# Two-layer hybrid backbone on one core: two-piece modulation steps, part of layer 1's modulation in its own mixer, last gathered products issued during expert selection

## The chip, the cores and the metric

The kernel runs on one core of a Trainium2 chip. The metric is the device time of one execution in microseconds (us); the median of several runs is compared. The engines are TensorE (PE: matmuls; PEld: its weight loads), VectorE (DVE), ScalarE (ACT), GpSimd (POOL) and SyncE (SP). DMA transfers are issued from queues that belong to engines: SP loads weights, ACT loads some activations, POOL issues the indirect transfers that gather rows by index.

## What is computed

Two layers over 256 latent tokens and 256 context tokens, width 1024, all in float32. Cut to what matters:

```python
mod = silu(c) @ w_mod[l] + b_mod[l]          # 6 vectors of 1024; one set for latent, one for context
h = rmsnorm(x) * (1 + scale1) + shift1       # mod 0, 1
x = x + mod[2] * token_mixers(h)             # one input projection, four mixers, merge, output projection
h = rmsnorm(x) * (1 + scale2) + shift2       # mod 3, 4
x = x + mod[5] * peer_ffn(h)                 # layer 0 also for the context tokens
def peer_ffn(t):                             # per token, 8 heads
    q = t @ w_q                              # product-key scores: two top-16, then top-16 of 256 sums
    e, g = chosen 128 experts, softmax gates
    act = gelu(u_tab[e] . t)
    return sum(g * act * v_tab[e])           # 16384 experts per layer
```

## The kernel before

The program is one list of items (class Item: a function and the weight pieces that it reads). `run` (line 92) goes through the list once and writes out the instructions of all engines in that order; each engine then executes its own instructions in order. Ahead of each item `load` (line 100) issues the next weight pieces of 512 KB on SP. Pieces that are cut into two fp32r halves go through three `raw` buffers; pieces with a `ring` name go, in order, through the buffers of `self.ring`, as soon as `ring_for` has their name and a buffer is free. `cut` (line 167) makes the halves on ACT and on DVE or POOL. FIRST (line 71) is the item before which no cut is made ahead of need.

**Modulation** (`mod_items`, line 322). `w_mod` of a layer is 48 pieces: three groups (group 0: vectors 0 and 1; group 1: 2 and 3; group 2: 4 and 5), four quarters q, four pieces kp. One piece is one step: two matmuls with 512 columns (line 356), each of which writes 32 of the 128 partitions of a PSUM tile psM; the profile shows two records for each matmul. After four steps ACT copies the row (line 363), TensorE transposes it (line 334), and DVE adds it up (lines 336 to 346). Layer 0: group 0 runs at the start of the program, groups 1 and 2 are woven among the input products and scans of its mixer (line 988) through a ring of four buffers. Layer 1: all 48 steps stand in layer 0's expert stage, woven among six query products and the first nine up steps (line 1550), through four buffers.

**Expert stage** (`peer`, line 1005). The latent tokens (in layer 1 their last 160) take the dense way: every expert of the layer is multiplied with all of them. The other 256 (layer 0: the context tokens) or 96 tokens are "far": their chosen rows are gathered. The order is:

- Seven query items (`wq`, line 1101), with the head scores and top-k on DVE beside them.
- 128 up steps (`up`, line 1312): eight matmuls (line 1318) with a piece of `peer_u`, and GELU on ACT. Beside them, as *row products*: POOL gathers one row of `u_rows` per token into a buffer of 512 KB (line 1217), and DVE multiplies and adds it up against the tokens (line 1248), 256 times in layer 0, 96 in layer 1, with six other buffers fetched ahead in layer 0.
- N/4 selection items (`experts`, line 1354; 64 in layer 0, 40 in layer 1): one-hot matrices from ACT, DVE and POOL (`one_hots`, line 1328; lines 1343 to 1349), four products that place the gates (line 1361), and a DVE product (line 1363).
- 128 down steps (`down`, line 1475; products of line 1498 in layer 1, of `mm3`, lines 200 to 202, in layer 0) with `peer_v`. The far tokens' down part (`far_down`, line 1376) gathers four rows at a time and needs eight matmuls (line 1409, psC) per step; 64 steps in layer 0, 24 in layer 1. EARLY (line 84) of these steps are spread over the selection items: 24 in layer 0, none in layer 1.

What stands beside an item is set by a budget written out by hand. `routing` (line 1276) is a generator that yields the cost of each thing that it issues (1.3 for a row product, 0.1 + n/700 for one top-k instruction on n values, and so on); `aside` (line 1303) adds the item's allowance to `due` and draws from the generator until `due` is used up. The allowances are WQ = 8.0 per query item and UP = 4.3 per up step in layer 0, 3.5 and 1.9 in layer 1. In `beside`, SHARE (0.75 in layer 0) is the part of other routing work that is drawn for each product. At up step 111 the own tokens' gates must be complete; at up step 127 of layer 0 all that is left is issued (1e6). Line 1290 lets `routing` wait, before the first row product of layer 0, until all 48 modulation steps are issued:

```python
            while two and hold["mods"] < 48:
                yield None
```

In layer 0, `far_steps` begins with selection item 0; in layer 1 after the last one. The transpose of line 1259, which follows the last row product of a tile, stands in TensorE's order where the budget puts it.

Of the kernel before, what the change touches and what calls it, by code (L numbers as in the profile page):

```python
# [6 lines left out]
F = mybir.dt.float32  # L7
# [62 lines left out]
class Builder:  # L70
    RAW, CUT, AGE, FIRST = 3, 5, 2, 20
# [12 lines left out]
    FAR, WQ, UP, SHARE, EARLY = (256, 96), (8.0, 3.5), (4.3, 1.9), (0.75, 0.6), (24, 0)  # L84
# [237 lines left out]
    def mod_items(self, l, groups, tag=("O", 1), turn=("T", 2), rows=("u", 1), ring="mix"):  # L322
# [25 lines left out]
        def fn(g, q, kp):  # L348
            def go(p):
                if kp == 0:  # L350
                    hold["ps"] = self.ps.tile([128, 512], F, tag=tag[0], name="psM", bufs=tag[1])
                ps = hold["ps"]
# [5 lines left out]
                if kp == 3:  # L358
                    row, (rt, n) = [], rows
                    for i in range(n):  # L360
                        w = 512 // n
                        rw = self.mp.tile([128, w], F, tag=rt, name="row", bufs=2)
                        nc.scalar.activation(rw, ps[:, i * w:i * w + w], AF.Copy)
# [3 lines left out]
        return [Item(fn(g, q, kp), Piece(self.t["w_mod"][l, g, q, kp], 1024, split=False, ring=ring))  # L367
                for g in groups for q in range(4) for kp in range(4)]

# [39 lines left out]
    def mixer(self, l, need):  # L409
# [14 lines left out]
        def begin():  # L424
# [42 lines left out]
        def ring_end():  # L467

            del self.ring[4:]
            self.ring_for = "mix"  # L470
# [497 lines left out]
        if l == 0:  # L968
            m = self.mod_items(l, (0,), tag=("A", self.BANKS["A"]), turn=("T", self.BANKS["T"]), ring="start")
            seq += m[:1] + [Item(stats1)] + m[1:4]  # L970
            seq += [Item(lambda: squares_end(0, 4)), m[4], Item(norm1), norm_steps(2)]
            seq += m[5:9] + [norm_steps(2)]
            seq += m[9:13] + [norm_steps(2)] + m[13:] + [Item(ring_end), self.lo(l, 0), Item(self.flush), norm_steps(3)]
# [5 lines left out]
        mods = self.mod_items(l, (1, 2), tag=("T", self.BANKS["T"]), turn=("T", self.BANKS["T"])) if l == 0 else []  # L979
# [25 lines left out]
    def peer(self, l, seg, far):  # L1005
# [270 lines left out]
        def routing():  # L1276
# [13 lines left out]
            while two and hold["mods"] < 48:  # L1290
                yield None
# [6 lines left out]
            yield from r  # L1298

# [12 lines left out]
        def up(i):  # L1312
            def fn(p):
# [7 lines left out]
                aside(self.UP[l] if i < 127 or not two else 1e6, "own" if i == LAST - 1 else None)  # L1321
# [31 lines left out]
        def experts(t4):  # L1353

            def fn():
# [184 lines left out]
        if l < L - 1:  # L1540
            def one(it):
                def fn(p):
                    it.fn(p)
                    hold["mods"] += 1
                    if hold["mods"] == 48:
# [119 lines left out]
```

## Time and profile before

| what | us |
|---|---|
| median of 3 runs (lowest, highest) | 3461.22 (3460.14, 3463.15) |
| profiled execution, its own time | 3454.95 |
| span of it, first to last instruction | 3453.2 |

Layer 0's mixer takes the span up to about 780, its expert stage to 2190 (up steps to 1493, selection to 1682, down steps to 2190), layer 1's mixer to 2690, its expert stage to 3453 (up steps to 3053, selection to 3109). The profile was taken in one execution. "Busy" is the time in which an engine had an instruction under way; an arrow in a row of waits points to what ended the wait; "x" is a count of records. Matmul ends are modelled and overlap, so the distance of starts tells more than one record's length. DMA share is the mean over the core's 16 DMA engines.

### The profile page before, as it was taken

What the parts mean: (1) busy time and instruction counts of PE and PEld (TensorE: products, weight loads), DVE (VectorE), ACT (ScalarE), POOL (GpSimd) and SP (SyncE); (2) the same over time, 40 slices, a digit from 0 to 9 for tenths busy, and PEclk for the clock granted to TensorE, in tenths of its full rate; (3) what the DMA queues carried; (4) which work ended last, traced back from release to release, by engine and by line L of the source; (5) the groups of instructions that cost most, each with busy time, mean ns of one, the idle gap of its engine ahead of it and who ended that gap; (6) DMA issues with size and microseconds to landing.
All of it is one profiled execution on the core that took longest, in us unless ns stands there. A gap on an engine that the chain in (4) does not pass through costs nothing. (4 is left out here: it accounts for less than half of the span.)

```text
span 3453.2 us, 50801 instructions
## 1 busy us (share of the span) xinstructions
PE 3152.3 (91%) x19130; PEld 2516.4 (73%) x19130; DVE 1890.9 (55%) x4591; ACT 1073.5 (31%) x2268; POOL 1259.8 (36%) x1178
## 2 busy tenths in 40 slices
PE   7999999997879999678888999899999899989998
PEld 4667766785458877543566889777878799888887
DVE  5557444445389999655433446677444767670001
ACT  4544444331101011034332335564454110160000
POOL 2422222220044445557434550344454033473330
PEclk9999999998989999899999999999999999999999
DMA  7522212334789999968778996523234699939996
GB/s 262 168 89 62 64 57 65 92 110 160 262 314 369 386 371 395 408 232 277 251 282 324 393 395 195 164 86 92 84 107 146 201 348 409 404 133 361 378 376 213
DMA packets 245013, 819.03 MB, mean 237 GB/s; under 512 B 31776, under 2 KB 50464, under 8 KB 244512
## 3 DMA queue, kind: packets, MB, share of 16 engines
q1 hardware_dynamic: 137824, 441.40, 36.8%
q0 software_dynamic: 101376, 369.14, 28.6%
q10 hardware_dynamic: 5568, 5.24, 0.5%
q8 instruction: 151, 2.47, 0.3%
q14 instruction: 94, 0.77, 0.1%
HBM read 809.37 MB, written 6.29 MB: 236 GB/s over the span
## 5 line engine op out<-in xcount | busy, mean ns | idle before, releaser
L178 POOL TENSOR_TENSOR whl<-raw,whl 128x512 fp32r<-128x512 f32 x249 | 325.7, 1323 | 829.9 <-ACT whl L174 764.5
L1318 PE MATMUL psA<-hb,raw 128*128 128x256 f32 x2048 | 474.2, 391 | 12.9 <-DMA raw<-peer_u 9.4
L176 DVE TENSOR_TENSOR whl<-raw,whl 128x512 fp32r<-128x512 f32 x359 | 272.5, 767 | 375.3 <-ACT whl L174 311.2
L174 ACT ACTIVATE whl<-raw 128x512 fp32r<-128x512 f32 x608 | 362.7, 627 | 322.0 <-PE acc L202 241.4
L1318 PEld LDWEIGHTS psA<-hb,raw 128*128 128x128 f32 x2048 | 394.0, 196 | 90.5 <-issue 19.1
L200 PE MATMUL psA<-hhi,whl 128*128 128x512 f32 (+1 forms) x1032 | 376.4, 365 | 10.0 <-ACT hhi L504 5.3
L202 PE MATMUL psA<-hhi,whl 128*128 128x512 f32 (+1 forms) x1032 | 364.2, 353 | 2.7 <-DVE whl L176 2.4
L201 PE MATMUL psA<-hlo,whl 128*128 128x512 f32 (+1 forms) x1032 | 365.4, 354 | 1.3 <-POOL hlo L505 1.2
L1217 POOL DMA_INDIRECT fetched<-u_rows,ft x184 | 184.1, 1001 | 333.5 <-DVE ft L1176 142.1
L200 PE MATMUL acc<-wh,whl 128*128 128x256 f32 x1024 | 295.3, 288 | 2.9 <-ACT wh L205 2.9
L201 PE MATMUL acc<-wh,whl 128*128 128x256 f32 x1024 | 290.8, 284 | 2.2 <-DVE wh L206 2.2
L202 PE MATMUL acc<-wh,whl 128*128 128x256 f32 x1024 | 290.4, 284 | 0.0
L1320 ACT ACTIVATE A<-psA 128x512 f32<-128x512 f32 (+1 forms) x128 | 66.2, 517 | 721.1 <-PE psA L1318 615.4
L1248 DVE SCALAR_TENSOR_TENSOR fetched<-fetched,hT 128x1024 f32<-128x1024 f32 x184 | 222.0, 1210 | 31.6 <-DMA fetched<-u_rows,ft 17.8
L200 PEld LDWEIGHTS psA<-hhi,whl 128*128 128x128 f32 x1032 | 198.5, 192 | 54.6 <-issue 18.7
L200 PEld LDWEIGHTS acc<-wh,whl 128*128 128x128 f32 x1024 | 197.2, 193 | 38.1 <-issue 14.9
L202 PEld LDWEIGHTS psA<-hhi,whl 128*128 128x128 f32 x1032 | 198.1, 192 | 30.4 <-DVE whl L176 3.6
L201 PEld LDWEIGHTS psA<-hlo,whl 128*128 128x128 f32 x1032 | 197.9, 192 | 27.5 <-POOL hlo L505 1.8
L1217 POOL DMA_INDIRECT hb<-peer_v,ft x140 | 145.6, 1040 | 176.0 <-PE psC L1409 142.1
L201 PEld LDWEIGHTS acc<-wh,whl 128*128 128x128 f32 x1024 | 197.5, 193 | 2.4 <-DVE wh L206 2.4
L202 PEld LDWEIGHTS acc<-wh,whl 128*128 128x128 f32 x1024 | 197.4, 193 | 0.0
L1217 POOL DMA_INDIRECT own<-u_rows,ft x96 | 105.7, 1101 | 241.1 <-DMA fetched<-peer_u 97.8
(372 smaller groups left out, 6065.7 us busy)
## 6 DMA issues: line engine op xcount, KB each, us to landing
raw<-peer_u SPq DMA_DIRECT2D x176, 512.0 KB
raw<-peer_v SPq DMA_DIRECT2D x176, 512.0 KB
raw<-w_in SPq DMA_DIRECT2D x126, 512.0 KB
fetched<-peer_u SPq DMA_DIRECT2D x80, 512.0 KB
fetched<-peer_v SPq DMA_DIRECT2D x80, 512.0 KB
ring<-w_mod SPq DMA_DIRECT2D x72, 512.0 KB
raw<-w_branch SPq DMA_DIRECT2D x32, 512.0 KB
hb<-w_mod SPq DMA_DIRECT2D x24, 512.0 KB
```

The source lines that it names most:

```text
L174: nc.scalar.activation(hx, x, AF.Copy)
L176: nc.vector.tensor_sub(lx, x, hx.bitcast(F))
L178: nc.gpsimd.tensor_sub(lx, x, hx.bitcast(F))
L200: mm(ps, wh, xh, start=start, stop=False, skip_group_check=skip)
L201: mm(ps, wh, xl, start=False, stop=False, skip_group_check=skip)
L202: mm(ps, wl, xh, start=False, stop=stop, skip_group_check=skip)
L1217: nc.gpsimd.indirect_dma_start(out=buf, out_offset=None, in_=rows, in_offset=bass.IndirectOffsetOnAxis(ap=idx.bitcast(I32), axis=0))
L1248: nc.vector.scalar_tensor_tensor(b, b, 1.0, h, op0=OP.mult, op1=OP.mult, accum_out=f[:, 3, k:k + 1])
L1318: nc.tensor.matmul(ps[:, :N], p.raw[:, k * 128:k * 128 + 128], h32[:, k, off:], start=k == 0, stop=k == 7)
L1320: nc.scalar.activation(A[:, i - 1:i + 1, :], hold["ps"][:, :, :N], AF.Gelu_apprx_tanh)
```

## The change

- A modulation step takes two pieces and issues four matmuls, one for each quarter of the partitions; a group has 8 steps instead of 16.
- Layer 1's groups 1 and 2 move from layer 0's expert stage into layer 1's mixer, woven among its input products and scans as in layer 0, through a ring of two buffers (the tiles `ohi` and `olo`); the row is copied in two parts into tiles with the tag `u`. Group 0 stays, woven among the query items only; line 1290 waits for its 8 steps, and all up steps follow.
- UP of layer 0 is 4.0 instead of 4.3. At up step 127 the rest is no longer issued at once: selection items draw 2.5 each until the row products are through, and the last draws all. `far_steps` begins at the item at which they are through, and catches up by at most one step per item. EARLY of layer 1 is 6 instead of 0, so that six of its 24 far down steps stand in the selection.
- FIRST is 14 instead of 20.

```diff
-    RAW, CUT, AGE, FIRST = 3, 5, 2, 20
+    RAW, CUT, AGE, FIRST = 3, 5, 2, 14
-    FAR, WQ, UP, SHARE, EARLY = (256, 96), (8.0, 3.5), (4.3, 1.9), (0.75, 0.6), (24, 0)
+    FAR, WQ, UP, SHARE, EARLY = (256, 96), (8.0, 3.5), (4.0, 1.9), (0.75, 0.6), (24, 6)
...
-        def fn(g, q, kp):
-            def go(p):
+        def fn(g, q, half):
+            def go(*ps):
...
-                for e in range(2):
-                    k = 2 * kp + e
-                    c = k % 4
-                    nc.tensor.matmul(ps[32 * c:32 * c + 32, :], self.sc[:, k, :], p.raw[:, e * 512:e * 512 + 512],
-                                     start=k < 4, stop=k >= 4)
+                for c in range(4):
+                    nc.tensor.matmul(pm[32 * c:32 * c + 32, :], self.sc[:, 4 * half + c, :],
+                                     ps[c // 2].raw[:, c % 2 * 512:c % 2 * 512 + 512], start=half == 0, stop=half == 1)
...
             else:
+                self.ring = [mp.tile([128, 1024], F, tag=tag, name="ring", bufs=2) for tag in ("ohi", "olo")]
+                self.ring_for = "mix1"
                 for d in (0, 4):
                     nc.scalar.dma_start(out=xt[:, d:d + 4, :C], in_=self.hc[:, d:d + 4])
...
-        mods = self.mod_items(l, (1, 2), tag=("T", self.BANKS["T"]), turn=("T", self.BANKS["T"])) if l == 0 else []
+        mods = self.mod_items(l, (1, 2), tag=("T", self.BANKS["T"]), turn=("T", self.BANKS["T"]),
+                              rows=("u", 2 - need, nb["u"]), ring=f"mix{l}")
...
-            while two and hold["mods"] < 48:
+            while two and hold["mods"] < 8:
                 yield None
...
             yield from r
+            hold["up"] = True
...
-                aside(self.UP[l] if i < 127 or not two else 1e6, "own" if i == LAST - 1 else None)
+                aside(self.UP[l], "own" if i == LAST - 1 else None)
...
-                if not two:
-                    aside(1.5 if t4 < N // 4 - 1 else 1e6)
-                if t4 == (0 if two else N // 4 - 1):
-                    hold["far"], hold["done"] = far_steps(), 0
-                if "far" in hold:
-                    far_go(EARLY * (t4 + 1) // (N // 4 - 4) if two else 1)
+                last = t4 == N // 4 - 1
+                if "up" not in hold:
+                    aside(1e6 if last else 2.5)
+                if "up" in hold:
+                    if "far" not in hold:
+                        hold["far"], hold["done"] = far_steps(), 0
+                    far_go(EARLY if last else min(hold["done"] + 1, EARLY * (t4 + 1) // (N // 4 - 4)))
...
-            first += [up(i) for i in range(9)]
             first = first[:1] + weave(first[1:], [one(it) for it in self.mod_items(
-                l + 1, (0, 1, 2), ("H", 1), ("A", 2), ("t0", 2), f"mod{l}")]) + [up(i) for i in range(9, 128)]
+                l + 1, (0,), ("H", 1), ("A", 2), ("t0", 2, 2), f"mod{l}")]) + [up(i) for i in range(128)]
```

## Rows read from the trace of the kernel before

**Rows 1.** The page: busy time of the engines, and DMA share in 40 slices.
```profile
PE 3152.3 (91%) x19130; PEld 2516.4 (73%) x19130; DVE 1890.9 (55%) x4591; ACT 1073.5 (31%) x2268; POOL 1259.8 (36%) x1178
...
DMA  7522212334789999968778996523234699939996
```

**Rows 2.** Stretches: us; PE, PEld, DVE, ACT, POOL busy; clock; DMA share; GB/s.
```profile
795.00:901.00 106.00, 89.49 (x421) 61.17 (x421) 65.95 (x243) 14.40 (x36) 0.00 (x0) 0.94 0.45 151
901.00:965.00 64.00, 56.40 (x277) 32.55 (x276) 4.42 (x28) 10.35 (x22) 6.82 (x7) 1.00 0.86 309
965.00:1300.00 335.00, 301.35 (x1340) 250.28 (x1340) 324.10 (x871) 28.75 (x45) 162.42 (x158) 0.94 0.97 365
1300.00:1366.00 66.00, 64.63 (x298) 53.72 (x296) 65.14 (x173) 6.06 (x9) 33.17 (x32) 1.00 1.01 397
1366.00:1476.00 110.00, 71.16 (x305) 59.19 (x305) 82.03 (x140) 9.51 (x17) 56.45 (x60) 0.85 0.98 388
...
1493.00:1682.00 189.00, 151.61 (x897) 75.90 (x895) 108.38 (x243) 92.38 (x252) 136.27 (x133) 0.97 0.81 278
...
2210.00:2325.00 115.00, 108.62 (x528) 85.71 (x528) 84.58 (x107) 78.29 (x124) 51.31 (x40) 0.96 0.31 87
...
3053.00:3109.00 56.00, 44.37 (x322) 38.46 (x320) 54.83 (x113) 51.90 (x149) 54.65 (x39) 1.00 0.05 17
3109.00:3437.00 328.00, 327.00 (x2430) 288.39 (x2431) 10.92 (x38) 2.06 (x5) 90.22 (x95) 1.00 0.92 346
```

**Rows 3.** Timeline: start, length, engine; first gather and first row product of layer 0.
```profile
901.90 1.16 POOL L1217 DMA_INDIRECT fetched<-u_rows,ft  x1 [142.09 <-DVE ft L1176]
...
965.12 1.22 DVE L1248 SCALAR_TENSOR_TENSOR fetched<-fetched,hT 128x1024 f32<-128x1024 f32 x1 [8.48 <-PE hT L1232]
```

**Rows 4.** Waits of PE, 1360 to 1500: us in total, times, longest.
```profile
PE psN L1259 <- DVE ft L1257: 31.3, 1, 31.3
```

**Rows 5.** Groups of PE's instructions, 52 to 330: busy, mean ns, idle before.
```profile
L356 PE MATMUL psM<-ring,sc 128*32 128x512 f32 x128 | 27.2, 604 | 0.0
...
L334 PE MATMUL psT<-ident,row 128*128 128x128 f32 x32 | 4.9, 275 | 2.0 <-ACT row L363 2.0
```

**Rows 6.** Timeline of PE: a modulation step alone, and two steps side by side.
```profile
113.91 1.05 PE L356 MATMUL psM<-ring,sc 128*32 128x512 f32 x4
114.89 0.50 PE L200 MATMUL psA<-hhi,whl 128*128 128x512 f32 x1
...
844.15 1.07 PE L356 MATMUL psM<-ring,sc 128*32 128x512 f32 x8
```

**Rows 7.** Timeline of PE: head scores of the top-k and eight up steps.
```profile
1309.85 0.49 PE L1147 MATMUL psS<-A 64*128 64x128 f32 x4
1310.27 3.72 PE L1318 MATMUL psA<-hb,raw 128*128 128x256 f32 x16
...
1314.35 28.77 PE L1318 MATMUL psA<-hb,raw 128*128 128x256 f32 x128
```

**Rows 8.** Timeline: last row product, first early gather, end of the third early step.
```profile
1475.00 1.21 DVE L1248 SCALAR_TENSOR_TENSOR fetched<-fetched,hT 128x1024 f32<-128x1024 f32 x1
...
1495.39 1.03 POOL L1217 DMA_INDIRECT hb<-peer_v,ft  x1 [0.17 <-issue]
...
1520.21 1.91 PE L1409 MATMUL psC<-hb,wl 128*32 128x512 f32 x10 [0.52 <-DMA hb<-peer_v,ft]
```

**Rows 9.** Chain that ended last: start, length, a load of 512 KB.
```profile
2687.80 6.01 DMA fetched<-wq
```

**Rows 10.** POOL in the selection stages: layer 1, layer 0 (two rows), both (min/median/max ns).
```profile
L1348 POOL TENSOR_SCALAR oi<-iota,sel 128x128 f32<-128x128 f32 x34 | 49.5, 1469 | 0.0
...
L1217 POOL DMA_INDIRECT hb<-peer_v,ft x45 | 49.7, 1105 | 12.2 <-issue 10.9 <-DVE oi L1348 0.9 <-PE psG L1361 0.3
...
L1348 POOL TENSOR_SCALAR oi<-iota,sel 128x128 f32<-128x128 f32 x29 | 29.2, 1007 | 21.3 <-PE psG L1361 14.3 <-ACT oi L1345 3.8 <-ACT oi L1343 1.9
...
L1348 POOL TENSOR_SCALAR oi<-iota,sel x72: 790/1467/1584, 1467.6 to 3105.3; 128x128 f32<-128x128 f32 x72
```

**Rows 11.** Timeline of PE: one far down step in layer 1's down stage.
```profile
3131.93 1.92 PE L1409 MATMUL psC<-own,wl 128*32 128x512 f32 x16
```

More of the change, by code (lines that the diff above doesn't have):

```diff
@@ L319, in x_in, with mod_items @@
         return self.t["x"][seg] if l == 0 else self.xs[seg]
-    def mod_items(self, l, groups, tag=("O", 1), turn=("T", 2), rows=("u", 1), ring="mix"):
+    def mod_items(self, l, groups, tag=("O", 1), turn=("T", 2), rows=("u", 1, 2), ring="mix"):
         nc = self.nc
@@ L346, in columns @@
                     self.vec[:, l, n + 2 * q:n + 2 * q + 2][:, :, None].to_broadcast([128, 2, 2]), op0=OP.add, op1=OP.mult)
-        def fn(g, q, kp):
-            def go(p):
-                if kp == 0:
+        def fn(g, q, half):
+            def go(*ps):
+                if half == 0:
                     hold["ps"] = self.ps.tile([128, 512], F, tag=tag[0], name="psM", bufs=tag[1])
-                ps = hold["ps"]
-                for e in range(2):
-                    k = 2 * kp + e
-                    c = k % 4
-                    nc.tensor.matmul(ps[32 * c:32 * c + 32, :], self.sc[:, k, :], p.raw[:, e * 512:e * 512 + 512],
-                                     start=k < 4, stop=k >= 4)
-                if kp == 3:
-                    row, (rt, n) = [], rows
+                pm = hold["ps"]
+                for c in range(4):
+                    nc.tensor.matmul(pm[32 * c:32 * c + 32, :], self.sc[:, 4 * half + c, :],
+                                     ps[c // 2].raw[:, c % 2 * 512:c % 2 * 512 + 512], start=half == 0, stop=half == 1)
+                if half == 1:
+                    row, (rt, n, nb) = [], rows
                     for i in range(n):
                         w = 512 // n
-                        rw = self.mp.tile([128, w], F, tag=rt, name="row", bufs=2)
-                        nc.scalar.activation(rw, ps[:, i * w:i * w + w], AF.Copy)
+                        rw = self.mp.tile([128, w], F, tag=rt, name="row", bufs=nb)
+                        nc.scalar.activation(rw, pm[:, i * w:i * w + w], AF.Copy)
                         row += [rw[:, c * 128:c * 128 + 128] for c in range(w // 128)]
@@ L366, in fn @@
             return go
-        return [Item(fn(g, q, kp), Piece(self.t["w_mod"][l, g, q, kp], 1024, split=False, ring=ring))
-                for g in groups for q in range(4) for kp in range(4)]
+        return [Item(fn(g, q, half), *[Piece(self.t["w_mod"][l, g, q, 2 * half + e], 1024, split=False, ring=ring)
+                                       for e in range(2)])
+                for g in groups for q in range(4) for half in range(2)]
     def statistics(self, ps, x, k, tmp):
@@ L469, in ring_end @@
             del self.ring[4:]
-            self.ring_for = "mix"
+            self.ring_for = "mix0"
         sq = {}
@@ L969, in mixer @@
             m = self.mod_items(l, (0,), tag=("A", self.BANKS["A"]), turn=("T", self.BANKS["T"]), ring="start")
[L970 to L973, printed above, removed]
+            seq += m[:1] + [Item(stats1)] + m[1:2]
+            seq += [Item(lambda: squares_end(0, 4)), m[2], Item(norm1), norm_steps(2)]
+            seq += m[3:5] + [norm_steps(2)]
+            seq += m[5:7] + [norm_steps(2)] + m[7:] + [Item(ring_end), self.lo(l, 0), Item(self.flush), norm_steps(3)]
         else:
@@ L1541, in one, with fn @@
             def one(it):
-                def fn(p):
-                    it.fn(p)
+                def fn(*p):
+                    it.fn(*p)
                     hold["mods"] += 1
-                    if hold["mods"] == 48:
+                    if hold["mods"] == 8:
                         self.later(self.ring.clear)
```

## The prediction

> **What bounds the kernel now.** I read the page first: the matmul queue is busy 91% of the span and the DMA slices are full only in some stretches [rows 1]. So most stretches follow TensorE, and the question is where they do not. The table of stretches answers it [rows 2]. In layer 0's expert stage (795 to 1682) four things alternate. Up to 965 DVE is nearly idle after 901 (4.4 of 64 us) although its long job, 256 row products, lies ahead. From 965 to 1366 DVE is busy 389 of 401 us and DMA 97 to 101%, so the gathered rows set the pace. From 1366 to 1476 TensorE falls to 71 of 110 us while DMA stays at 98%. From 1493 to 1682 (selection) TensorE works 152 of 189 us. In layer 1's mixer TensorE is busy 109 of 115 us at the start (2210 to 2325) with DMA at 31%. In layer 1's selection stage (3053 to 3109) DVE, ACT and POOL are all over 90% busy and DMA is at 5%; in the stage behind it TensorE has no gap (327 of 328 us).
>
> Two rows show what the change touches. The first gather is issued at 901.90, but the first row product runs at 965.12 [rows 3]: line 1290 lets no product be issued before all 48 modulation steps, so 63 us of DVE pass. And at the end TensorE waits 31.3 us in one piece on line 1259, the transpose behind the last product [rows 4]; four up steps stand behind it.
>
> **The change part by part.** The times are made against the profiled execution itself: 3454.95 us, of which the span is 3453.2. It lies 6.3 us below the median of the runs shown, so the sum is also taken off 3461.22. About 0.2% (7 us) is what a measurement of this kernel can tell from no change.
>
> *Layer 0's mixer, pairs to fours.* 32 modulation steps use 27.2 us of TensorE (128 records, four to a step) [rows 5]. A step alone holds it from 113.91 to 114.89, 0.98 us; eight records side by side, which is the new step, take 1.07 us from first start to last end, hardly more than the 1.05 of four [rows 6]. So a new step costs the same 0.98, 16 of them 15.7 us: -11.5 us where TensorE is full, 0 if the coarser step opens new waits. I take -11. At the start of the program the same 16 pieces arrive over the same queue, and the first step needs two of them instead of one: 0, between -2 and +4. FIRST 20 to 14 only keeps the first cuts at the same place among fewer steps; nothing.
>
> *Layer 0's expert stage, head.* 19 modulation pairs and four transposes between the query products become 8 fours and four transposes; some pairs already stood side by side. -2 us (0 to -5), which is kept only if the last query product still ends the top-k chain.
>
> *The row products start earlier.* The condition is now 8 steps, all issued before the last query product. A row needs a few us from issue to arrival, so the first product moves from 965 to about 904. From there, with counts from the costs in the code: budget 7 x 8 + 128 x 4.0 = 568, against four top-k (59.9 each), 256 products (1.3 each) and about 15 of small work = 587. So 14 products are left at the end of the up steps, and the own tokens' top-k ends at up step 110 with 192 products issued (before: step 102, also 192). Up to there the same DVE work lies ahead, 389 us. TensorE needs 109 up steps at 28.77/8 = 3.60 us and some 24 head scores at 0.42 net [rows 7]: about 407 us with transposes. DMA moves 198 rows and 106 pieces of 0.524 MB, 159 MB: 402 us at 397 GB/s, 437 at the 365 of 965 to 1300. The three floors are close together, so I take 407 plus the 3% by which before stood above its DVE floor (401 against 389): 420 us, ending at 1324 instead of 1366. Then 64 products remain in both kernels. They took 110 us at full DMA; now 8 fewer up pieces (4 MB, 10 us) compete, and DVE adds eight selection items of 1.9 us, under cover: 103 us. Last product at 1427 instead of 1476: -49.
>
> *The tail beside selection.* TensorE no longer stands 31.3 us behind the last product: the transpose is issued in selection item 7, so the last four up steps and items 0 to 6 run before it. Before, 19.2 us lay between the last product and the first fetch of the early down steps (1475.0 + 1.2 to 1495.4), and three early steps were done at 1522.1 [rows 8], with 10 items. Now the first fetch follows the last product by some 2 us and three steps catch up one per item in the same 26.7 us, with 11 items done. That is 19 - 2 + 3 = 20 us more. Against it stands nothing on the path but the products themselves, which are counted above. Sum of this stage -49 - 20 = -69; with the rounding of the start I take -68, between -42 (10% of friction in the first part) and -95 (no friction, row rate at its best). After that, early steps and down steps are as before.
>
> *Layer 1's mixer takes 16 steps.* 16 x 0.98 + 8 x 0.6 for the transposes (32 records, 4.9 us [rows 5]) = 20.5 us in a stretch that is 94% full. Their pieces go through a ring of two buffers, so a pair loads only after the step before it has run. A load of this kind took 6.01 us on the chain, with others beside it [rows 9]; 16 steps over 115 + 20 us stand 8.5 us apart. About four steps behind a short product wait 1 to 2 us: +6. Each ring load waits on SP for TensorE, and the w_in loads queue behind it; they are two to three pieces ahead of their use, which covers it. Row copies (ACT) and reductions (DVE) have room there. Less 2 us of gaps filled: +24, between +12 and +60. In the expert stage their removal saves nothing more than is counted.
>
> *Layer 1's selection.* Products are all issued by up step 124 in both kernels, so the new item is EARLY = 6: six steps with 24 gathers move from the down stage into 40 selection items. Down loses 6 x 1.92 = 11.5 us of TensorE, all of it on the path. In selection POOL already runs back to back at 1.469 us per item [rows 10]. A gather costs it 1.105 + 0.27 = 1.38 us, 24 of them 33 us. The POOL operation took 1.007 us where DVE was 57% busy (layer 0), 0.79 at its shortest: as the items get longer, DVE thins out. 40 x 1.007 + 33 = 73 us instead of 59: +14.5 - 11.5 = +3 (psC row [rows 11]); with 0.79, -6; with 1.469 kept, +21.
>
> **Sum:** -11 - 2 - 68 + 24 + 3 = -54: 3401 against its own 3455, **3407** against the median.
>
> **The rivals.**
> *POOL stays slow in layer 1's selection.* For it: 1.469 us each, without a gap, beside a DVE that is 98% busy [rows 2, 10]. If DVE holds POOL back as much as now, the gathers add their full 33 us: +21 instead of +3, 3425. Against it: 1.007 us in layer 0. The Trainium skill, "SBUF — State Buffer", section "Who interferes with whom", states a rule that speaks for this rival: a VectorE instruction with two SBUF inputs and a GpSimd instruction that reads SBUF exclude one another for the whole instruction. By that rule POOL would keep its 1.47 us as long as such DVE instructions stay dense; the trace agrees with a stretch from 0.79 to 1.47, and does not show what happens once POOL is the later one.
> *Gathers stay at 365 GB/s.* The first part then takes 437 x 1.03 = 450 us, 30 more: 3437. For it: 0.97 share over 335 us [rows 2].
> *The three engines overlap better.* 407 us, and 95 for the rest: 3386.
> *Layer 1's mixer waits for its ring (slower).* If the weave puts steps so close, or SP comes to the ring load so late, that each step waits for a whole load, 16 x 6.0 = 96 us come in place of the 6 allowed: 3497. It decides from 54/16 = 3.4 us of wait per step beyond the 0.4 allowed. Against it: 8.5 us between steps, DMA at 31%.
> That the tail is not moved at all can be excluded by the count above: 587 against 568.
>
> **How the numbers follow.** Forecast 0.45, POOL slow 0.15, 365 GB/s 0.18, better overlap 0.16, ring 0.06. The range 3370 to 3448 takes in the second to fourth case and most of the bounds of -68 and +24; outside lie the ring case and pairs of bad cases (above), or of good ones (below). Slower by over 0.2%: the ring case without its mild end, 0.05. Within 0.2%: that end, and 365 GB/s together with slow POOL and a few ring waits, 0.03. Faster: 0.92.
>
> **What would show it.** Right: 16 modulation steps in layer 0's scan part, the first row product near 904, no wait of 30 us on line 1259, early gathers from about 1430; the start of layer 1's mixer 20 to 30 us longer, with a few waits of line 356 for DMA; layer 1's selection near 73 us and its down stage 11 shorter. Wrong: a first product near 904 but a last one near 1476 (DMA was the bound); waits of several us for DMA at each modulation step of layer 1; selection of layer 1 near 90 us.

## The result, and the profile after

| what | us |
|---|---|
| before, median of 4 runs (lowest, highest) | 3460.68 (3458.02, 3463.15) |
| after, median of 4 runs (lowest, highest) | 3425.52 (3421.81, 3428.33) |
| profiled execution after, its own time; span | 3428.33; 3426.6 |

The ratio is 0.9898, 95% interval 0.9881 to 0.9915: faster by 35 us, 1.0%. The forecast was 54. The profiled execution after lies 2.8 us above its median and the one before 5.7 below its own, so between the two traces the gain is only 26.6 us; the rest is scatter between runs.

Two parts of the page after, busy time and DMA share in 40 slices, against [rows 1]:

```profile
PE 3136.2 (92%) x19130; PEld 2516.7 (73%) x19130; DVE 1892.8 (55%) x4591; ACT 1077.7 (31%) x2268; POOL 1245.3 (36%) x1178
...
DMA  7432222234699999887789966542335699969995
```

The number of matmul records is the same (19130): a two-piece step issues the matmuls of two old steps side by side. Only their place and their waits changed. The stretches after, with the columns of [rows 2]:

```profile
899.00:1300.00 401.00, 393.88 (x1827) 329.89 (x1826) 387.17 (x1038) 39.60 (x62) 196.18 (x192) 1.00 1.00 393
1300.00:1364.00 64.00, 61.75 (x283) 52.46 (x281) 44.18 (x76) 10.41 (x22) 32.88 (x35) 1.00 1.02 407
1364.00:1408.00 44.00, 14.62 (x58) 12.46 (x56) 41.90 (x79) 11.21 (x29) 29.40 (x30) 0.56 0.97 371
1408.00:1599.00 191.00, 146.01 (x842) 70.28 (x842) 110.96 (x239) 82.66 (x226) 134.35 (x131) 0.94 0.81 278
2129.00:2293.00 164.00, 144.93 (x703) 96.66 (x703) 95.22 (x140) 88.06 (x147) 50.65 (x41) 0.93 0.51 164
3017.00:3093.00 76.00, 54.94 (x405) 44.37 (x403) 58.48 (x119) 53.07 (x149) 65.69 (x63) 0.91 0.54 179
3093.00:3411.00 318.00, 317.81 (x2358) 287.25 (x2359) 9.71 (x36) 2.75 (x6) 67.79 (x71) 1.00 0.88 318
```

From 899 to 1300 TensorE (394 of 401 us busy), DVE (387) and DMA (share 1.00) are all full, so the lost head of the expert stage is used. The next two stretches are the tail: TensorE has 15 us of work in 44 us, DMA is still full. The mixer of layer 1 (2129 to 2293) has become 164 us long where it was 119.5 between the same two instructions (2209.7 to 2329.2).

Where the time went, from marks in the two traces. Each mark is the start of an instruction, so that the differences add up:

| section | before | after | change | forecast |
|---|---|---|---|---|
| layer 0's mixer, to the first query product | 795.7 | 792.0 | -3.7 | -11 |
| to the last query product | 81.2 | 76.9 | -4.3 | -2 |
| to layer 0's first down product | 805.1 | 729.9 | -75.2 | -68 |
| down products | 507.8 | 509.0 | +1.2 | 0 |
| layer 1's mixer, to its first query product | 507.1 | 552.8 | +45.7 | +24 |
| to layer 1's last up product | 356.0 | 356.7 | +0.7 | 0 |
| selection and down of layer 1 | 385.4 | 393.9 | +8.5 | +3 |

The rows sum to -27.1; -26.6 is the difference of the two times, with 0.5 behind the last down product. Layer 0 came out slightly better than forecast and layer 1's mixer cost almost twice as much. The first gather and the first row product, against [rows 3] (timeline of all engines):

```profile
893.87 1.16 POOL L1219 DMA_INDIRECT fetched<-u_rows,ft  x1 [136.47 <-PE psA L1321]
...
899.02 1.22 DVE L1250 SCALAR_TENSOR_TENSOR fetched<-fetched,hT 128x1024 f32<-128x1024 f32 x1 [1.82 <-PE psA L1321]
```

The first product runs 5 us behind the first gather instead of 63. The last one starts at 1415.2 (before 1475.0), the first early gather at 1408.3 (1495.4), and the first down product at 1598.8 (1682.0).

The waits of TensorE in the two stretches from 1360 to 1599 (total us, times, longest) show what took the place of [rows 4]:

```profile
PE psG L1364 <- DVE oj L1352: 30.3, 8, 6.7
...
PE psC L1413 <- DMA hb<-peer_v,ft: 19.5, 29, 1.7
```

Of the wait of 31.3 us on the transpose 6.4 are left (at 1417.28), but eight selection items now wait 30.3 us for a one-hot matrix of DVE, which DVE builds only between row products. The wait changed its name, not its size.

Layer 1's mixer, 2129 to 2293: the group of the moved modulation products (busy, mean ns, idle before) and TensorE's waits:

```profile
L354 PE MATMUL psM<-ring,sc 128*32 128x512 f32 x128 | 25.6, 674 | 11.1 <-DMA ring<-w_mod 11.1
```
```profile
PE psM L354 <- DMA ring<-w_mod: 11.1, 6, 3.4
PE psT L334 <- ACT row L361: 3.4, 2, 2.9
```

### The profile page after: what moved, and what is told of

Read it like the earlier page. It is cut to its first block, busy times and chain, and to the rows that moved or that the text cites. A ratio compares the mean times of both kernels' runs of the same rounds, so it can differ in the third digit from the quotient of the medians.

```text
span 3426.6 us, 50779 instructions
## 1 busy us (share of the span) xinstructions
PE 3136.2 (92%) x19130; PEld 2516.7 (73%) x19130; DVE 1892.8 (55%) x4591; ACT 1077.7 (31%) x2268; POOL 1245.3 (36%) x1178
## 5 line engine op out<-in xcount | busy, mean ns | idle before, releaser
L1321 PE MATMUL psA<-hb,raw 128*128 128x256 f32 x2048 | 458.5, 383 | 9.1 <-DMA raw<-peer_u 7.0
L1321 PEld LDWEIGHTS psA<-hb,raw 128*128 128x128 f32 x2048 | 383.9, 190 | 76.7 <-issue 8.1
L1250 DVE SCALAR_TENSOR_TENSOR fetched<-fetched,hT 128x1024 f32<-128x1024 f32 x184 | 221.1, 1208 | 20.5 <-DMA fetched<-u_rows,ft 18.5
```

Of the source, the lines that this page charges most:

```text
L1250: nc.vector.scalar_tensor_tensor(b, b, 1.0, h, op0=OP.mult, op1=OP.mult, accum_out=f[:, 3, k:k + 1])
L1321: nc.tensor.matmul(ps[:, :N], p.raw[:, k * 128:k * 128 + 128], h32[:, k, off:], start=k == 0, stop=k == 7)
```

## The experiments

Twelve kernels, four runs of each and ten of e9. "Changed" is the kernel after. e1, e3, e4 and e7 ran on one chip, e5, e6, e8 and e9 on a second, e10 to e13 on a third; the ratio is always to the kernel before on the same chip, which had medians of 3458.31, 3461.28 and 3460.53 us. e12 is the changed kernel once more: its trace has 549.5 us for layer 1's mixer and 397.5 for the selection and down stage of layer 1, where the table above has 552.8 and 393.9, so differences of 4 us between single traces say little.

| kernel | median (lowest to highest), us | ratio, 95% interval |
|---|---|---|
| e1: ring of four | 3411.03 (3409.79 to 3414.65) | 0.9865, 0.9844 to 0.9887 |
| e3: rest issued at once, as before | 3426.71 (3423.55 to 3432.99) | 0.9913, 0.9889 to 0.9937 |
| e4: nothing moved | 3431.59 (3423.91 to 3431.82) | 0.9914, 0.9890 to 0.9938 |
| e7: the 16 steps left out | 3382.91 (3377.31 to 3386.59) | 0.9784, 0.9762 to 0.9806 |
| e5: ring of four, one early step in layer 1 | 3407.41 (3401.92 to 3412.99) | 0.9842, 0.9820 to 0.9863 |
| e6: FIRST 20 | 3436.46 (3433.06 to 3448.83) | 0.9928, 0.9910 to 0.9946 |
| e8: ring of four, EARLY (16, 1) | 3379.30 (3368.97 to 3387.38) | 0.9763, 0.9734 to 0.9792 |
| e9: before with UP 4.0 | 3441.32 (3435.01 to 3459.97) | 0.9945, 0.9930 to 0.9959 |
| e10: ring of four, EARLY (16, 0) | 3368.13 (3364.66 to 3368.66) | 0.9727, 0.9706 to 0.9747 |
| e11: ring of four, EARLY (8, 0) | 3400.79 (3395.60 to 3406.33) | 0.9829, 0.9804 to 0.9853 |
| e12: changed, unaltered | 3422.72 (3420.74 to 3427.30) | 0.9891, 0.9869 to 0.9912 |
| e13: FIRST 20, beside e12 | 3431.67 (3424.18 to 3436.34) | 0.9912, 0.9886 to 0.9937 |

**Layer 1's mixer: are the steps dear, or their ring?** e1 lends the ring two more buffers from a tile that lies idle in that stretch; e7 leaves the steps out (its two vectors are constants, zero and one).

```diff
             merged = mp.tile([128, 8, N], F, name="merged")
+            if l:
+                self.ring += [merged[:, a:a + 4].rearrange("p x y -> p (x y)") for a in (0, 4)]
```


> Layer 1's mixer loads its modulation pieces through four ring buffers instead of two (the tile of the merged branches, idle in that part, gives two more); all else as in the changed kernel. Theory A (the moved steps cost 45 us instead of 24 because pairs arrive late and TensorE's clock falls in these waits): the waits of line 354 for DMA in layer 1's mixer, 11.1 us on PE, fall to 2 or less, the stretch from the second first-product half to the first attention score falls from 164.4 to about 148 us, and the whole to about 3410. Rival B (the steps cost what they take on TensorE and in the engines behind it, the waits only change their name): less than 4 us, about 3423.

```diff
-                              rows=("u", 2 - need, nb["u"]), ring=f"mix{l}")
+                              rows=("u", 2 - need, nb["u"]), ring=f"mix{l}") if l == 0 else []
```


> Leaves out layer 1's modulation groups 1 and 2 altogether (no loads, no products; the vectors are zero and the gain one), so its output is not the reference's; all else as in the changed kernel. It measures the price of the 16 moved steps with everything that hangs on them. Theory A: 43 to 47 us less than the changed kernel, about 3380, all of it between the end of layer 0's down steps and layer 1's first attention score. Rival B (the longer mixer has another cause than the steps, such as a later start of its inputs): less than 30 us.

From the end of the down stage to layer 1's first query product it is 552.8 us in the changed kernel, 532.2 in e1 and 505.3 in e7. So in this stretch the steps as such cost 27 us and the ring of two another 21. Theory A holds in both: the waits are the ring's, and all 16 steps together are worth 42.6 us in the medians (47.5 between the marks), just under the 43 to 47 of e7. Of the ring's 21 us the medians show 14.5, or 9 to 12 when each kernel is taken against the kernel before on its own chip; in e1's trace layer 0's down stage and layer 1's last stage are 4 us longer each. In e1 TensorE has no wait for a ring load left; its longest entry in that stretch, 2128 to 2272, is another:

```profile
PE psT L590 <- ACT r L592: 6.7, 3, 4.4
```

The stretch is 20 us shorter (144 against 164). The waits that vanish are 11.1 us, but others grew, so TensorE's idle time falls by 8.5. The rest is busy time: in nearly the same records TensorE is busy 133.47 us in e1 against 144.93 after (stretch, e1):

```profile
2128.00:2272.00 144.00, 133.47 (x695) 94.06 (x699) 92.62 (x136) 85.17 (x141) 50.08 (x41) 0.96 0.55 183
```

The timeline of TensorE in the changed kernel shows where (start, length, [idle before]); the first row and the last two follow the three longest waits for the ring:

```profile
2146.74 1.07 PE L354 MATMUL psM<-ring,sc 128*32 128x512 f32 x4 [3.40 <-DMA ring<-w_mod]
2148.28 1.92 PE L354 MATMUL psM<-ring,sc 128*32 128x512 f32 x4 [0.47 <-DMA ring<-w_mod]
2150.14 5.84 PE L588 MATMUL psT<-u,lw 128*128 128x512 f32 x8
2176.13 3.13 PE L354 MATMUL psM<-ring,sc 128*32 128x512 f32 x8 [3.16 <-DMA ring<-w_mod]
2250.15 3.56 PE L354 MATMUL psM<-ring,sc 128*32 128x512 f32 x8 [3.20 <-DMA ring<-w_mod]
```

Behind the first wait the second half of a step takes 1.92 us where the first took 1.07, and eight products of line 588 take 5.84 us, 730 ns each beside a mean of 609 in e1. Behind the others a whole step takes 3.13 and 3.56 us, where [rows 6] has 1.07. In these places the granted clock is low (stretches of the changed kernel and, second fence, of e1; the clock is the third number from the end):

```profile
2138.00:2147.00 9.00, 5.61 (x45) 4.31 (x46) 5.41 (x4) 2.84 (x6) 6.10 (x5) 1.00 0.69 220
2147.00:2155.00 8.00, 7.53 (x15) 2.28 (x12) 0.00 (x0) 3.32 (x5) 0.00 (x0) 0.57 0.67 213
2155.00:2174.00 19.00, 17.46 (x103) 12.37 (x101) 13.84 (x18) 14.18 (x22) 8.35 (x8) 1.00 0.40 139
2174.00:2182.00 8.00, 5.87 (x22) 3.21 (x23) 6.58 (x13) 0.42 (x1) 1.18 (x1) 0.57 0.67 222
2182.00:2250.00 68.00, 62.49 (x317) 43.86 (x315) 40.57 (x55) 40.88 (x65) 25.36 (x22) 1.00 0.50 163
2250.00:2254.00 4.00, 3.56 (x8) 0.38 (x8) 3.79 (x7) 0.24 (x1) 0.84 (x1) 0.57 0.72 219
```
```profile
2136.00:2176.00 40.00, 35.80 (x226) 25.53 (x225) 29.58 (x36) 24.78 (x43) 19.38 (x15) 1.00 0.63 219
2176.00:2181.00 5.00, 4.81 (x15) 2.00 (x16) 0.42 (x1) 2.64 (x6) 0.46 (x1) 0.66 0.67 172
2181.00:2272.00 91.00, 85.21 (x424) 59.64 (x427) 56.41 (x84) 53.06 (x85) 29.80 (x26) 1.00 0.49 167
```

A mean of 0.57 over 8 us is mostly half speed (1.2 GHz) with a little full speed (2.4 GHz) at the edges. The clock falls three times, each time at the end of a wait of 3.2 to 3.4 us for the ring, and is 1.00 between; the one fall in e1 follows its wait of 4.4 us for ACT. (From 2130 to 2138 it is low too, 0.57, but so it is in e1 from 2128 to 2136, 0.58: that is not the ring's.) Length times the missing share of the clock is 8.6 us in the three stretches and 1.7 in e1's one, so by this estimate the clock takes about 7 of the 11.5 us; the other 4 to 5 were not placed. And the reason for the wait is on SP's queue in the changed kernel:

```profile
2141.62 0.33 SPq L113 DMA_DIRECT2D raw<-w_in  x1
2142.05 0.86 SPq L107 DMA_DIRECT2D ring<-w_mod  x2
2145.65 0.33 SPq L113 DMA_DIRECT2D raw<-w_in  x1
2147.85 2.73 SPq L107 DMA_DIRECT2D ring<-w_mod  x2
```

A step runs at 2139.67, its two buffers come free, the two loads for the next step are issued at 2142.05, in SP's order behind a load of `w_in`, and that step, due at 2143.35, starts at 2146.74. With two buffers and two pieces to a step, no load can start before the step ahead of it has run.

**Did the move pay?** e4 keeps the 24 two-piece steps in layer 0's expert stage, so that the row products wait for all of them.

```diff
-                              rows=("u", 2 - need, nb["u"]), ring=f"mix{l}")
+                              rows=("u", 2 - need, nb["u"]), ring=f"mix{l}") if l == 0 else []
...
-            while two and hold["mods"] < 8:
+            while two and hold["mods"] < 24:
...
+            first += [up(i) for i in range(9)]
-                l + 1, (0,), ("H", 1), ("A", 2), ("t0", 2, 2), f"mod{l}")]) + [up(i) for i in range(128)]
+                l + 1, (0, 1, 2), ("H", 1), ("A", 2), ("t0", 2, 2), f"mod{l}")]) + [up(i) for i in range(9, 128)]
```


> All 24 steps of layer 1 stand in layer 0's expert stage as before the change (woven among six query products and nine up steps, row products wait for all of them), in the new two-piece form; the tail, UP 4.0 and EARLY as in the changed kernel. Theory A (the move gains about 45 us in the expert stage through the earlier row products and gives about 45 us back in layer 1's mixer, so it is worth little by itself): first row product between 940 and 960, layer 1's mixer 45 us shorter, the whole between 3418 and 3438. Rival B (the move is the gain of this change, as the prediction had it, 61 us for 24): about 3455 or more.

In e4 the first row product starts at 953.2 and the first down product of layer 0 at 1654.1, 55.3 us later than after; layer 1's mixer takes 502.5 us, 50.3 less. Both directions of the move are about as large as each other: it is worth 5 us by these two marks, 6 in the medians, as theory A had it. Between 27 us (e4 beside its own chip's kernel before, 3458.31) and 29 of the 35 come without it. In e4 the first row product starts 11.9 us earlier than before (965.1) although all 24 steps still stand ahead of it: that part comes from the two-piece steps.

**Where do those come from?** e9 takes the kernel before and changes one constant; e3 takes the tail out of the changed kernel; e6 and e13 put FIRST back.

```diff
-    FAR, WQ, UP, SHARE, EARLY = (256, 96), (8.0, 3.5), (4.3, 1.9), (0.75, 0.6), (24, 0)
+    FAR, WQ, UP, SHARE, EARLY = (256, 96), (8.0, 3.5), (4.0, 1.9), (0.75, 0.6), (24, 0)
```


> The kernel before with one number changed: UP of layer 0 is 4.0 instead of 4.3, so that 14 products are issued at the last up step and not before it. Theory A (of the 80 us that layer 0's expert stage gained, some 15 come from this number: the transpose behind the last product no longer has four up steps behind it): the first early gather follows the last product by about 5 instead of 19 us, the first down product moves from 1682 to about 1667, the whole to about 3445. Rival B (slower pacing delays the products by as much): within 4 us of before, about 3456.

By the medians UP 4.0 alone is worth 20 us (3441.32 against 3461.28). The profiled execution of e9 was the slowest of its ten (3459.97), and in it the first down product of layer 0 starts at 1681.8, not at the 1667 of theory A; so no trace shows where the 20 us lie. What the trace does show is the order of the instructions. TensorE around the last row product, e9:

```profile
1429.74 7.57 PE L1318 MATMUL psA<-hb,raw 128*128 128x256 f32 x34
1483.68 0.47 PE L1259 MATMUL psN<-ident,ft 128*128 128x128 f32 x1 [46.37 <-DVE ft L1257]
1483.95 6.21 PE L1361 MATMUL psG<-oi,oj 128*128 128x128 f32 x34
```

The transpose now stands behind all up products, not ahead of the last four. TensorE waits longer than in [rows 4] (46.4 us), but with nothing of the up stage behind the wait; the first early gather follows the last row product by 5.3 us (1481.7, 1487.0) instead of 20.4. In this trace the last product itself comes 6.7 us later than before, and from the first early gather to the first down product it is 194.8 us instead of 186.6, which uses the gain up.

```diff
-                aside(self.UP[l], "own" if i == LAST - 1 else None)
+                aside(self.UP[l] if i < 127 or not two else 1e6, "own" if i == LAST - 1 else None)
```


> Up step 127 of layer 0 again issues all row products that are left, so that none stand beside selection; all else as in the changed kernel. Theory A (the tail is worth the wait behind the last product and the eight selection items that run in it): TensorE waits again 30 us or more in one piece on the transpose behind the last product, the first down product of layer 0 moves from 1598.8 to about 1619, and the whole to about 3445. Rival B (selection is bound by its 24 early gathers, about 7.5 us each, wherever it begins, and items beside the products gain nothing): the first down product within 6 us, about 3429.

Theory A fell. The one long wait is back in e3, and it costs at most 3 us:

```profile
PE psN L1261 <- DVE ft L1259: 45.1, 1, 45.1
```

The last product is at 1405.7, 9.5 us earlier than after, with no selection work between the products on DVE; the first early gather is at 1411.0 against 1408.3, and the first down product at 1601.7 against 1598.8, as Rival B had it. From the first early gather to the first down product it is 186.6 us before, 190.5 after, 190.7 in e3, 187.5 in e4, 187.1 in e1, and 193.5 at most in the other kernels with 24 early steps (e9's 194.8 apart): nearly the same, whether selection items are done ahead or not. So the 24 early steps should set that length, not the 64 items; e8, e10 and e11 below test it.

> The changed kernel with FIRST 20 as before. Theory A (the edit is worth nothing, as predicted; layer 0's mixer gained 4 us and not 11 because the single steps had covered waits for ACT): within 3 us of the changed kernel, about 3425, first query product of layer 0 within 2 us of 792. Rival B (cutting from item 14 on puts ACT's cuts ahead of its evictions and ate 7 us): first query product near 785, about 3418.

> The changed kernel with FIRST 20 instead of 14, as e6, beside the unaltered changed kernel on the same chip. Theory A: layer 0's mixer gained only through FIRST 14, so e13 is 3 to 6 us over e12 and its first layer-0 query product starts at about 795 us. Rival B: e6's 11 us over the changed kernel were the work of FIRST as a whole (also beyond the mixer): 9 to 13 us over e12. Rival C: they were that chip's, and e13 equals e12 within 2 us.

Both kernels have the one edit `FIRST = 20`. e6 is 11 us slower than the changed kernel was on another chip, which neither of its theories had; so it was repeated. (In e6's trace the row products take 526.4 us from first to last, in e5's and e8's on the same chip 523.6 and 522.5, but 515 to 517 in the like kernels on the other two chips, so up to 10 of the 11 us may be that chip's.) Beside e12 it is 9.0 us: C falls, and by the median it is at the lower edge of B. In the traces of e12 and e13 the first query product is at 789.4 and 794.7, so 5.3 of 8.5 us lie in the mixer, as A has it; the rest has no one place and was not settled. TensorE's waits in the first 260 us of e13 name the cause, which e12 does not have:

```profile
PE psA L200 <- ACT whl L174: 4.8, 1, 4.8
```

With eight items instead of sixteen in group 0, item 20 lies later in the work than before, so the first cut comes too late. FIRST 14 does not gain; it keeps the two-piece steps from losing 5 us.

**The early steps.** If 24 early steps set layer 0's selection, fewer must shorten it; and in layer 1 even the six may be too many. EARLY counts draws from `far_down`, and the first draw only fetches the rows of the first step. So EARLY 6 in layer 1 puts the products of five steps into the selection, not of six (80 psC records stand there after), and EARLY 1 puts none there: it only draws the fetch of the first four rows at item 35 (of 0 to 39) instead of at the last. The edits of e5, e8, e10 and e11 are the ring of e1 and EARLY: (24, 1), (16, 1), (16, 0) and (8, 0). In e8 (layer 0), e10 and e11 the last selection item draws one step more; in layer 1 with EARLY 0 that is the one fetch that the kernel before also draws there. The diff of e10:

```diff
-    FAR, WQ, UP, SHARE, EARLY = (256, 96), (8.0, 3.5), (4.0, 1.9), (0.75, 0.6), (24, 6)
+    FAR, WQ, UP, SHARE, EARLY = (256, 96), (8.0, 3.5), (4.0, 1.9), (0.75, 0.6), (16, 0)
...
-                    far_go(EARLY if last else min(hold["done"] + 1, EARLY * (t4 + 1) // (N // 4 - 4)))
+                    far_go(EARLY + 1 if last else min(hold["done"] + 1, EARLY * (t4 + 1) // (N // 4 - 4)))
```


> The kernel with four ring buffers in layer 1's mixer, and in layer 1 only the first fetch (EARLY 1 instead of 6) beside selection. Theory A (the six early steps in layer 1 cost more on POOL than they save in the down stage: 18.7 against 10.1 us in the traces): layer 1's selection back from 76 to about 58 us, its down stage 10 us longer, the whole 8 to 9 us below the kernel with four ring buffers (3411), about 3402. Rival B (the prediction's sum, +3 for the six steps): 3408.

> As the kernel with four ring buffers and EARLY 1 in layer 1, but with 16 early steps beside layer 0's selection instead of 24 (the last item draws up to 17, so that the step that frees the cut buffers still lies ahead of the down steps, as it does with 24). Theory A (after the first early gather, selection lasts as long as its gathers: 187 to 191 us in every kernel so far, 7.8 us a step, whatever ran before it): from the first early gather to the first down product about 130 to 140 us instead of 188, eight steps of 1.9 us more in the down stage, the whole 25 to 40 us lower, about 3370. Rival B (the far steps are bound by their gathers in the down stage too, so what selection gives up the down stage takes): the end of layer 0's down steps within 8 us of the other kernel, about 3400.

> The changed kernel with the ring of four buffers in layer 1 and EARLY (16, 0): layer 0 as in e8, layer 1 without early gathers, as in the kernel before. Theory A: early gathers in layer 1's selection cost their POOL time there and are not paid back (last up product to end 385.4 us in the kernel before, 392.2 with one early step), so the time is about 7 us under e8's 3379.3, about 3372, and last up product to end is 384 to 386 us. Rival B: what the selection gives up the down stage takes back; the time stays at 3376 to 3382.

> As e10 with EARLY (8, 0): half as many early gathers in layer 0's selection. Theory A: with 16 early steps the selection is still set by their gathers (138.2 us for 16 steps in e8, 8.6 us a step), so 8 steps take about 100 to 110 us, until the items themselves bind, while the down stage grows by less (from 506 us at 24 early steps to 531 at 16, 3.1 us a step): 10 to 15 us under e10, about 3360. Rival B: with 8 the items bind already (about 120 us) or the down stage, now short of products, grows by 5 us a step and more: e10's time or up to 20 us above it.

Layer 1, last up product to last down product: 385.4 us before and 385.3 in e10 (fetch at the last item), 392.2 in e5 and 392.1 in e8 (fetch at item 35), 393.9 after, 398.2 in e1, 395.7 in e3 (EARLY 6). Early gathers there lose, and already the first four do. e5's median, 3407.41, had not settled this, as its expectation had both theories within 6 us of each other; e10 has Theory A's number. POOL in that selection, after and, second fence, in e10:

```profile
L1351 POOL TENSOR_SCALAR oi<-iota,sel 128x128 f32<-128x128 f32 x37 | 37.5, 1019 | 23.7 <-ACT A L1323 21.6 <-PE psG L1364 1.8
L1219 POOL DMA_INDIRECT own<-peer_v,ft x20 | 22.9, 1147 | 5.1 <-issue 3.0 <-PE psG L1364 0.9 <-DVE oi L1351 0.9
```
```profile
L1353 POOL TENSOR_SCALAR oi<-iota,sel 128x128 f32<-128x128 f32 x37 | 52.9, 1441 | 23.2 <-ACT A L1325 23.2
```

Why four gathers cost that much is on POOL's timeline, of e5 and, second fence, of e10:

```profile
3055.76 1.53 POOL L1221 DMA_INDIRECT own<-peer_v,ft  x1 [0.16 <-issue]
...
3060.42 0.94 POOL L1221 DMA_INDIRECT own<-peer_v,ft  x1 [0.30 <-issue]
3061.40 1.58 POOL L1353 TENSOR_SCALAR oi<-iota,sel 128x128 f32<-128x128 f32 x2
```
```profile
2997.46 23.31 POOL L1353 TENSOR_SCALAR oi<-iota,sel 128x128 f32<-128x128 f32 x16
3020.94 1.53 POOL L1221 DMA_INDIRECT own<-peer_v,ft  x1 [0.16 <-issue]
```

In e5 the four gathers hold POOL for 5.6 us ahead of the last two one-hot matrices; in e10 they stand behind all of them. From the last up product to the first down product it is 61.7 us in e5 and e8, 57.0 in e10. The other 2 us are in the down stage (330.5 and 330.4 against 328.3) and were not explained.

Layer 0, from the first early gather to the first down product and from there to the last, with the shares of DMA (second last number): e12 (24 steps), e10 (16), e11 (8):

```profile
1406.00:1594.00 188.00, 147.07 (x842) 71.28 (x842) 110.38 (x239) 82.59 (x225) 133.97 (x130) 0.94 0.82 284
1594.00:2104.00 510.00, 485.04 (x3736) 396.99 (x3735) 233.22 (x410) 199.55 (x340) 159.09 (x156) 0.97 0.82 299
```
```profile
1406.00:1545.00 139.00, 106.70 (x714) 63.76 (x714) 105.90 (x234) 80.90 (x226) 104.17 (x96) 0.94 0.77 255
1545.00:2076.00 531.00, 506.22 (x3864) 400.18 (x3864) 234.03 (x418) 198.96 (x339) 187.54 (x188) 0.98 0.86 321
```
```profile
1409.00:1527.00 118.00, 85.33 (x585) 63.25 (x585) 102.69 (x226) 79.30 (x226) 65.49 (x64) 0.85 0.47 153
1527.00:2106.00 579.00, 539.33 (x3992) 406.59 (x3992) 237.01 (x427) 200.41 (x341) 219.40 (x220) 0.98 0.87 324
```

From 24 to 16 steps the selection gives back 49 us (6.1 a step) and the down stage takes 21, more than the 15 of theory A of e8 (eight steps of 1.9), but far less than is given back, as that theory had it. From 16 to 8 it gives back only 21, 2.6 a step, so with 8 the early steps no longer set the selection alone, and the down stage takes 48, 6 a step: Rival B of e11, and beyond its bound (32.7 us above e10, where it allowed 20). Share times length, DMA works 572, 564 and 559 us in the three kernels, so nearly the same, and stands idle for 126, 106 and 138. With 24 steps TensorE waits for gathers in the selection; with 8, DMA is half idle there and its gathers fall into the down stage, where TensorE then waits for them (e11, 1527 to 2106):

```profile
PE psC L1415 <- DMA hb<-peer_v,ft: 30.1, 28, 2.7
PE psC L1415 <- DMA A<-peer_v,ft: 8.5, 9, 1.8
```

These are 38.6 us in e11; in e10 the same two waits are 20.3 and 2.3. TensorE's busy time in psC products grows by 31.5 us (from 128.1 to 159.6), twice what eight steps alone would take (15.4), so part of the waiting lies hidden in it. That the total of the bytes and not the number of row buffers makes these waits was not tested. Whether the best count is 16 or a neighbour of it was not tried. e10 is the fastest kernel of the study: 3368.13 us, 92 less than before and 55 less than e12.

## Why the prediction was right and wrong

The sign and the range (3370 to 3448) held; 3425.52 is 18.5 us above the forecast of 3407. That the rival with a slow POOL also has 3425 is an accident: POOL was not slow. Layer 0's sum was met (-82 against -81) in part by luck, since two of its terms missed in opposite directions and one came out for another reason. By its own steps, against the traces:

- **Layer 0's mixer, -11: mis-sized, -4 to -6.** The products became as cheap as said: the 128 records take 17.1 us where [rows 5] has 27.2, so -10.1. But the step allowed "0 if the coarser step opens new waits" and then took nothing for them. TensorE's idle time grew from 5.3 (52 to 242 us) to 11.8 us (52 to 240), in small waits on ACT: lines 635 and 588 wait 3.5 and 3.0 us where it was 0.7 and 1.1, and line 667 waits 1.5. "FIRST 20 to 14 ... nothing" was right as a difference, with the reason given; e13 shows the 5 us that it saves.
- **Head, -2: -4.3.** Within its 0 to -5.
- **The row products start earlier, -49.** The first product was forecast at 904 and came at 899.0; the end of the own tokens' weights was forecast at 1324 and came at 1305; the last product at 1427 and came at 1415. From the last query product the gain is 51.8 us. The rate of gathers was the doubt (365 GB/s); it was 393 from 899 to 1300, so that rival fell. The third rival, better overlap, held in this stretch (about 406 us from 899 to 1305, forecast 420, rival 407), while its total of 3386 was eaten up by layer 1.
- **The tail, -20: the number came out, the reason did not.** Last product to first down product fell from 207.0 to 183.6 us, 23 less. The step credited that to items 0 to 6 running ahead of the transpose and to early steps catching up. e3 undoes this and loses 3 us in the trace, 1 in the median. What counted is when the first early gather can be issued; from there it is 187 to 194 us in the kernels with 24 early steps, and 194.8 in e9. It was late in the kernel before because four up products' steps stood behind the wait of [rows 4], and UP 4.0 moves those ahead of it. The prediction used 4.0 only for counting products. By e3, which has 196.0 us from last product to first down product, the order is worth 11 of the 23; the other 12 come with the tail, which also puts the last product 9.5 us later. That the four up steps are the cause rests on the order in e9 and e3 and on e9's median.
- **Layer 1's mixer, +24: mis-sized, +46.** This step alone is 22 of the 27 us between forecast and trace. "About four steps behind a short product wait 1 to 2 us: +6" rested on 8.5 us between steps against 6.0 for a load [rows 9]. That compares a mean distance with one load. A step needs two loads, they start only when the step before has run, and steps are not evenly placed: six waits, 11.1 us. And behind the three longest of them the granted clock was lower, by estimate 7 us more; the prediction had no term for this. The Trainium skill, "TensorE: Matmul & The Clock Gate", section "HAM oscillation — how this bites in real kernels", tells of a kernel whose TensorE falls back to the lower clock at each wait for a slice of data. The trace agrees for the waits of 3.40, 3.16 and 3.20 us, with 0.57 behind each, and not for the one of 0.48 us at 2168.42, around which the clock is 1.00. With four buffers the step costs 27 us (e1 against e7), about what was said. The rest is the ring rival's mechanism at a fifth of its price (21 against 96), below its point of decision.
- **Layer 1's selection, +3: +8.5.** The stage was forecast at 73 us and took 75.9, from 57.1, not 59; the down stage gave 10.3 us, not 11.5, as five steps left it and not six (5 x 1.92 = 9.6). The disputed figure was POOL's operation: 1.007 us was taken, the rival had 1.469, and it measured 1.02. The rule of the Trainium skill, "SBUF — State Buffer", section "Who interferes with whom" (some VectorE and GpSimd instructions exclude one another), asked for dense DVE instructions to keep POOL at 1.47. Here DVE thinned out from 54.8 of 56 us to 58.5 of 76, and the operation fell to 1.02; with no early gather ahead of the last item (e10) it stays at 1.44. So the rule is not contradicted, and its condition went away as POOL became the later one. Still the trade loses 7 us and more: e10 with EARLY 0 has the 385.3 us of before.

The weak place in the chances is the ring case: at 0.06 it was priced only at its full 96 us. Its mild form, the 20 us that came, lay inside the step's own bounds (+12 to +60) but was no case by itself.

## What to carry to other kernels

A price for moved work holds only if its loads can be ahead: compare the distance between two uses with the whole chain (buffer free, issue, all loads of a step), not with one load, and give a ring at least twice what one step takes. Ask of every long wait what stands behind it in the queue: by the order in e3 and e9, the 31 us of wait cost about what the four up steps behind it took, and 45 us with nothing of the up stage behind it cost 3 us at most. When a stage does not shorten although its visible wait is gone, look for the count that it is built around (here 24 early steps), vary that, and measure the stage that receives what this one gives up.

## What was not expected of the hardware

- Three waits of 3.2 to 3.4 us for the ring were each followed by 4 to 8 us with a granted clock of 0.57; a wait of 0.48 us was not. Together with three short waits (11.1 us in all) they went with 11.5 us more of TensorE's busy time for nearly the same products, of which the clock explains about 7 by estimate.
- In the first 401 us of row products gathers and weight loads together held 393 GB/s with TensorE at a clock of 1.00. The kernel before had 365 in its first 335 us and 397 in the 66 us behind them [rows 2], so 365 was no limit of the transfers.
- Four gathers drawn four selection items earlier added 7 us to layer 1's selection and down stage (392.2 against 385.4) and moved no product. 4.7 of them are POOL's: the gathers stand ahead of the last two one-hot matrices.
